# Strassen's algorithm on a third row pair of eight in the first MLP product

## The chip, the cores and the metric

The kernel runs on one core of a Trainium2 chip. TensorE (PE in the profile) multiplies matrices, with its weight loads shown apart (PEld); VectorE (DVE) and ScalarE (ACT) do elementwise work; GpSimd (POOL) and SyncE (SP) mostly start DMA transfers. The metric is the device time of one execution in microseconds, lower is better; a time given for a kernel is the median of several runs.

## What is computed

A trunk of two layers over 256 tokens of width 2048, in float32. Each layer has an attention half and an MLP half; the change is in the MLP half:

```python
for l in range(DEPTH):                     # DEPTH = 2
    u = rmsnorm(x, norm_mix[l])
    ...                                    # two kinds of attention, gated and merged
    x = x + merged @ w_out[l]
    h = rmsnorm(x, norm_mlp[l]) @ w_ff1[l]          # 2048 -> 8192
    x = x + jnp.square(jax.nn.relu(h)) @ w_ff2[l]   # 8192 -> 2048
return rmsnorm(x, norm_final)
```

## The kernel before

**Precision.** Every float32 factor is split into a high part (rounded to the format that TensorE multiplies fast, by a cast on ScalarE) and a low part (the remainder, by a subtraction on VectorE). A product is then three matmuls: high by high, high by low, low by high. In the MLP half `parts` does the split of weights (L172 the cast, L173 the subtraction), into tiles `hi` and `lo` of which there are three each.

**The MLP half.** It goes through four blocks `b` (L775) of 2048 hidden columns. A block is four calls of `gemm_s` (L368): the first product for column half `g` = 0 and 1 (L788), then the second product for the output halves 0 and 1 (L806); in the last block the second half is done by `gemm_a` instead (L816). A call of `gemm_s` computes 256 rows by 1024 columns with 2048 contracted, in eight steps called row pairs: a pair `j` is 256 rows of the weight, one DMA of 1 MB into `raw` (L391, three buffers), against 2 x 2 blocks of the activations.

A plain pair casts its 128x2048 weights in one piece and does 8 block products of three matmuls each, 24 matmuls of 512 columns (L399, all matmuls on L383). They go into four PSUM banks, numbers 2, 3, 4 and 8. A pair named in `pairs` is done by Strassen's algorithm (in Winograd's form): VectorE builds four sums of the weight's quarters (`ts`, L405 to L411, one buffer), the three quarters that are used as they stand and the four sums are split (L412, L413, so two `hi` and two `lo` tiles in place of one), and there are 7 block products, 21 matmuls, into banks 1 to 7:

```python
w11, w22, w21 = cut(raw[:, 512:])
w1, w3, w2, w4 = cut(ts)
...
mm3(1, a11, l11, *w11)
mm3(2, a12, l12, *w21)
mm3(3, s4, r4, *w22)
mm3(5, s1, r1, *w1)
mm3(7, s3, r3, *w3)
mm3(6, s2, r2, *w2)
mm3(4, a22, l22, *w4)
```

The first three use the first `hi`/`lo` tile, the last four the second. All eight PSUM banks are in use in a call. At its end ScalarE copies bank 1 (L427) and VectorE adds the other banks up in eight additions (L428 to L435, recorded as L426) to four result tiles.

**Activations.** `turned_pair` (L339) transposes four 128x128 blocks on TensorE (L346) into a bank, takes them to SBUF (for hidden rows by ScalarE's square, L786), and splits them (L360, L361). For a pair that goes by Strassen it first forms four sums of 128x128 on VectorE (L352 to L355) and splits these too; its high and low parts then take four tiles from the pool `slots` in place of two. This is done once per layer for the eight pairs of normed rows (L758) and in every block for the eight pairs of hidden rows (L785). Pieces of such work are held as generators and handed out between the matmuls by `tick` (L125), a count of steps with due times; `drain` (L144, called at L404 ahead of the first Strassen pair) hands out all that is left.

**Order.** The program's own order gives priorities; a planner that knows the cost of instructions then fixes the order in each engine's queue when the kernel is built. At run time each queue goes in that order and waits on semaphores.

**Constants.** `FIRST` and `SECOND` (L65) name the Strassen pairs of the first and of the second product. `NSLOT` (L62) is the number of 128x512 tiles in `slots`, which hold activations, hidden rows and results. `SMALL` is the number of tiles of 128x256 tagged `small` (L96), which exist in the attention half alone: `whole` (L236) takes two to bring an accumulator out of PSUM (L238, L240), `rope` (L463) and `Norm.add` (L296) one each. A `slots` tile takes 2 KB of a partition, a small tile 1 KB.

Of the kernel before, what the change touches and what calls it, by code (L numbers as in the profile page):

```python
# [58 lines left out]

NSLOT, SMALL, RBUFS, HBUFS = 46, 8, 3, 4  # L62


FIRST, SECOND = (3, 5), (2, 4, 6)  # L65


SPACING, LAG1, LAG2 = 6, 13, 3
# [822 lines left out]
```

## Time and profile before

| | |
|---|---|
| median of 3 runs | 2675.92 us (2674.61 to 2676.1) |
| the profiled execution | 2675.85 us |
| its span, first to last instruction | 2674.1 us |
| instructions on TensorE, VectorE, ScalarE | 12606, 2172, 1611 |
| matmuls on L383, the MLP's `gemm_s` | 5538 (3692 with a high part, 1846 with a low part of the weight) |
| DMA traffic | 508.92 MB, 190 GB/s |

The profile is of one execution. Its rows give for each engine the line of the kernel, the tile written and the tiles read, the shape and the count; then the busy time, the mean of one in ns, and the time for which the engine stood idle just before such an instruction, with what ended the wait behind an arrow. A timeline row begins with the start in microseconds and the duration. The first layer's attention half lasts to 643.8 us, its MLP half from there to about 1338; the second layer follows in the same way.

### The profile page before, as it was taken

The page shows a single profiled execution, that of the slowest core. Times are in us where ns is not written, and L with a number is a line of the kernel's source. Part 1 is how long each engine was busy: PE and PEld are TensorE (multiplying, and loading weights), DVE is VectorE, ACT ScalarE, POOL GpSimd, SP SyncE. Part 2 cuts the span into 40 slices and gives each one's busy share as a digit, 9 for nine tenths or more (in the row PEclk, how much of TensorE's full clock was granted, in tenths as well). Part 3 has the DMA queues.
Part 4 walks back from the last instruction along what each step waited for, and adds up shares of the span by engine and source line. Part 5 has one row for each costly group of instructions (what it writes and reads, how often), then busy time and mean ns, then how long its engine had stood idle before and what let it go on. Part 6 is the DMA issues. An engine that isn't in the chain of part 4 may idle for free.

```text
span 2674.1 us, 31697 instructions
## 1 busy us (share of the span) xinstructions
PE 2636.0 (99%) x12606; PEld 2206.9 (83%) x12606; DVE 1912.9 (72%) x2172; ACT 1388.7 (52%) x1611; POOL 95.4 (4%) x122
## 2 busy tenths in 40 slices
PE   8999999999999999999999999999999999999998
PEld 7888888878888888888888888888788888888886
DVE  5675486556788887888667654955568888878885
ACT  5554464445555545546445544644455555455553
POOL 1100000000000010000001000000000000100000
PEclk9999999999999999999999999999999999999999
DMA  7555644555667585675555555455655665766754
GB/s 233 185 156 190 195 152 157 189 189 167 206 194 237 169 241 193 201 235 176 186 179 179 163 188 185 147 170 172 202 169 200 204 220 179 237 204 199 252 168 147
DMA packets 199301, 508.92 MB, mean 190 GB/s; under 512 B 13457, under 2 KB 17553, under 8 KB 199153
## 3 DMA queue, kind: packets, MB, share of 16 engines
q1 hardware_dynamic: 189184, 488.14, 55.6%
q0 software_dynamic: 8960, 17.14, 3.2%
q8 instruction: 98, 1.61, 0.2%
q10 hardware_dynamic: 1008, 1.61, 0.2%
q14 instruction: 51, 0.41, 0.0%
HBM read 492.18 MB, written 2.10 MB: 185 GB/s over the span
## 4 chain that ended last, share of the span: by engine, by line
PE 85%; issue 7%; DVE 5%; ACT 2%; DMA 1%; POOL 0%; POOLq 0%; DVEq 0%; ACTq 0%
PE bank L383 36%; PE bank L228 11%; PE bank L229 11%; PE bank L227 11%; PE bank L218 8%; PE bank L219 4%; DVE lo L173 2%; ACT hi L172 2%; PE bank L346 1%; PE bank L232 1%; PE bank L234 1%; PE bank L233 1%; DVE pair L361 1%; PE bank L496 0%; DMA raw<-in_w_in 0%
## 5 line engine op out<-in xcount | busy, mean ns | idle before, releaser
L383 PE MATMUL bank<-hi,pair 128*128 128x512 f32 x3692 | 1147.3, 390 | 4.3 <-ACT hi L172 3.3
L383 PEld LDWEIGHTS bank<-hi,pair 128*128 128x128 f32 x3692 | 691.8, 188 | 153.7 <-ACT hi L172 11.0
L173 DVE TENSOR_TENSOR lo<-raw,hi 128x2048 fp32r<-128x2048 f32 (+1 forms) x288 | 618.3, 2150 | 184.9 <-ACT hi L172 183.8
L172 ACT CAST hi<-raw 128x2048 fp32r<-128x2048 f32 (+1 forms) x288 | 517.5, 1802 | 442.0 <-PE bank L383 254.5
L383 PE MATMUL bank<-lo,pair 128*128 128x512 f32 x1846 | 720.0, 390 | 0.0
L197 DVE TENSOR_TENSOR lo<-raw,hi 128x1024 fp32r<-128x1024 f32 (+1 forms) x352 | 427.6, 1217 | 343.4 <-ACT hi L196 342.8
L196 ACT CAST hi<-raw 128x1024 fp32r<-128x1024 f32 (+1 forms) x352 | 364.5, 1041 | 402.9 <-PE bank L229 291.6
L228 PE MATMUL bank<-lo,pair 128*128 128x512 f32 (+1 forms) x1344 | 518.5, 386 | 2.4 <-DVE lo L173 2.4
L227 PE MATMUL bank<-hi,pair 128*128 128x512 f32 (+1 forms) x1344 | 518.9, 387 | 0.0
L229 PE MATMUL bank<-hi,pair 128*128 128x512 f32 (+1 forms) x1344 | 518.1, 386 | 0.0
L383 PEld LDWEIGHTS bank<-lo,pair 128*128 128x128 f32 x1846 | 346.6, 188 | 72.8 <-DVE lo L173 1.8
L218 PE MATMUL bank<-pair,hi 128*128 128x512 f32 x960 | 346.3, 403 | 4.2 <-ACT hi L196 3.8
L228 PEld LDWEIGHTS bank<-lo,pair 128*128 128x128 f32 x1344 | 253.4, 189 | 51.5 <-DVE lo L173 2.9
L229 PEld LDWEIGHTS bank<-hi,pair 128*128 128x128 f32 x1344 | 253.4, 189 | 50.7
L227 PEld LDWEIGHTS bank<-hi,pair 128*128 128x128 f32 x1344 | 253.1, 188 | 49.1
L219 PE MATMUL bank<-pair,lo 128*128 128x256 f32 x960 | 266.9, 282 | 0.0
L173 DVE TENSOR_TENSOR lo<-sums,hi 128x2048 fp32r<-128x2048 f32 x74 | 169.6, 2292 | 112.9 <-ACT hi L172 112.9
L172 ACT CAST hi<-sums 128x2048 fp32r<-128x2048 f32 x74 | 141.5, 1912 | 185.5 <-DVE sums L411 154.5
L218 PEld LDWEIGHTS bank<-pair,hi 128*128 128x128 f32 x960 | 181.2, 189 | 43.6 <-ACT hi L196 4.2
L219 PEld LDWEIGHTS bank<-pair,lo 128*128 128x128 f32 x960 | 181.9, 190 | 1.7
L426 DVE TENSOR_TENSOR wide<-wide,bank 128x512 f32<-128x512 f32 x240 | 153.9, 679 | 0.0
L407 DVE TENSOR_TENSOR sums<-raw 128x1024 f32<-128x1024 f32 x74 | 90.2, 1219 | 11.7 <-DMA raw<-in_w_ff 11.4
(122 smaller groups left out, 1463.6 us busy)
## 6 DMA issues: line engine op xcount, KB each, us to landing
raw<-in_w_ff SPq DMA_DIRECT2D x256, 1024.0 KB, 5.3
raw<-in_w_in SPq DMA_DIRECT2D x124, 1024.0 KB, 5.1
raw<-in_w_out SPq DMA_DIRECT2D x32, 1024.0 KB, 5.0
raw<-in_w_o_na SPq DMA_DIRECT2D x16, 1024.0 KB, 5.0
raw<-in_w_o_mla SPq DMA_DIRECT2D x16, 1024.0 KB, 5.0
xt<-wide POOLq DMA_DIRECT2D x48, 256.0 KB, 7.1
raw<-in_w_ukv SPq DMA_DIRECT2D x8, 1024.0 KB, 4.9
raw<-in_w_uq SPq DMA_DIRECT2D x8, 768.0 KB, 4.5
```

The costliest lines, as they stand in the source:

```text
L172: nc.scalar.copy(hi, src)
L173: nc.vector.tensor_tensor(lo, src, hi.bitcast(F32), op=ALU.subtract)
L196: nc.scalar.copy(hi, src)
L197: nc.vector.tensor_tensor(lo, src, hi.bitcast(F32), op=ALU.subtract)
L218: nc.tensor.matmul(ps, wh, a, start=first, stop=False)
L219: nc.tensor.matmul(ps[:, :S], wl, a[:, :S], start=False, stop=last)
L227: nc.tensor.matmul(ps, ah, wh, start=first, stop=False)
L228: nc.tensor.matmul(ps, ah, wl, start=False, stop=False)
L229: nc.tensor.matmul(ps, al, wh, start=False, stop=last)
L383: nc.tensor.matmul(b[i], x, y, start=count[i] == 1, stop=count[i] == total[i])
L407: nc.vector.tensor_tensor(ts[:, :1024].rearrange("p (a n) -> p a n", a=2), raw[:, :512].rearrange("p (a n) -> p a n", a=1).to_broadcast([P ...
L426: add = lambda o, a, c: nc.vector.tensor_tensor(o, a, c, op=ALU.add)
```

## The change

Pair 6 of the first product joins pairs 3 and 5 as a Strassen pair. Two constants move with it: two more tiles in `slots` and four fewer small tiles, the same 4 KB of a partition.

```diff
-NSLOT, SMALL, RBUFS, HBUFS = 46, 8, 3, 4
+NSLOT, SMALL, RBUFS, HBUFS = 48, 4, 3, 4
...
-FIRST, SECOND = (3, 5), (2, 4, 6)
+FIRST, SECOND = (3, 5, 6), (2, 4, 6)
```

`FIRST` is used at L759, where the normed rows of its pairs get their sums, and at L788, where `gemm_s` takes the pairs. No other line changes.

## The prediction

> **What bounds the kernel now.** I read the page first, then the busy time by stage, the chain of waits, and the queues of VectorE and ScalarE where that chain leaves TensorE. The page says how full TensorE is:
>
> ```profile
> span 2674.1 us, 31697 instructions
> PE 2636.0 (99%) x12606; PEld 2206.9 (83%) x12606; DVE 1912.9 (72%) x2172; ACT 1388.7 (52%) x1611; POOL 95.4 (4%) x122
> ```
>
> TensorE idles 38 us in all, but 99% is an average. By stage: one of the four MLP blocks of a layer (first line), and the up-projections of the latent attention (second):
>
> ```profile
> 864.50:1036.60 172.10, 171.55 (x772) 141.55 (x771) 141.63 (x128) 92.42 (x73) 7.07 (x8) 1.00 0.65 208
> ...
> 350.00:405.00 55.00, 54.23 (x369) 49.85 (x368) 53.08 (x126) 36.68 (x87) 0.00 (x0) 1.00 0.48 154
> ```
>
> The columns are the stretch, then busy time of PE, PEld, DVE, ACT and POOL, the granted clock (1.00) and the DMA share. In the MLP VectorE is busy 141.6 of 172.1 us; in the attention stretch 53.1 of 55.0, a second limit beside TensorE. The chain of waits prices a matmul and shows where TensorE isn't alone:
>
> ```profile
> 738.58 1.75 PE bank L346 x16
> ...
> 743.56 1.92 ACT hi L172
> ...
> 765.86 1.91 ACT hi L172
> ...
> 767.81 96.65 PE bank L383 x425
> ```
>
> 96.65 us over 425 matmuls is 0.227 us from one 512-column matmul to the next (one matmul's own duration is longer, since they overlap; the step is what counts). Sixteen transposes cost 1.75. A block has 2 x 186 + 2 x 183 = 738 matmuls of L383 and 32 transposes: 738 x 0.227 + 2 x 1.75 = 171.0 us of 172.1, so about 1.1 us of a block is waiting. It falls early in the second product, where the chain leaves TensorE and runs over ScalarE and VectorE, from 743.56 to 767.81. ScalarE's and TensorE's own rows there:
>
> ```profile
> 752.24 0.62 ACT L360 CAST pair<-f 128x512 fp32r<-128x512 f32 x1 [0.94 <-DVE f L354]
> 752.76 1.91 ACT L172 CAST hi<-sums 128x2048 fp32r<-128x2048 f32 x1
> ```
> ```profile
> 757.16 0.97 PE L383 MATMUL bank<-hi,pair 128*128 128x512 f32 x3 [0.42 <-ACT hi L172]
> ```
>
> A cast of sums stood behind a small cast that waited; TensorE then waited too.
>
> **What goes.** A Strassen pair takes 21 matmuls where a plain one takes 24. There are 2 layers x 4 blocks x 2 column halves = 16 such products, so 48 matmuls go: 48 x 0.227 = **10.9 us**, 0.68 per product. Nothing hides them: the stretch is full of them.
>
> The Trainium skill ("TensorE: Matmul & The Clock Gate", Back-to-back issue gap) gives about 131 ns per 512-column matmul in a sustained stream of weight loads and matmuls, and about 216 for isolated ones. By 131 the saving would be 6.3 us, by 216 10.4; the trace's 227 for this very instruction stands against the first and near the second.
>
> **What is added to each of the 16 products.** VectorE and ScalarE prepare pair 6 as two tiles in place of one:
>
> ```profile
> L173 DVE TENSOR_TENSOR lo<-raw,hi 128x2048 fp32r<-128x2048 f32 x22 | 50.3, 2286 | 9.3 <-ACT hi L172 9.2
> L173 DVE TENSOR_TENSOR lo<-sums,hi 128x2048 fp32r<-128x2048 f32 x10 | 22.9, 2292 | 15.1 <-ACT hi L172 15.1
> L426 DVE TENSOR_TENSOR wide<-wide,bank 128x512 f32<-128x512 f32 x32 | 20.5, 678 | 0.0
> L173 DVE TENSOR_TENSOR lo<-raw,hi 128x1536 fp32r<-128x1536 f32 x10 | 17.5, 1752 | 2.1 <-ACT hi L172 2.1
> L407 DVE TENSOR_TENSOR sums<-raw 128x1024 f32<-128x1024 f32 x10 | 12.2, 1219 | 1.6 <-DMA raw<-in_w_ff 1.6
> L411 DVE TENSOR_TENSOR sums<-raw,sums 128x512 f32<-128x512 f32 x11 | 7.6, 688 | 0.2
> L361 DVE TENSOR_TENSOR pair<-f,pair 128x512 fp32r<-128x512 f32 x11 | 7.4, 686 | 2.0 <-ACT pair L360 2.0
> ```
> ```profile
> L172 ACT CAST hi<-raw 128x2048 fp32r<-128x2048 f32 x22 | 42.1, 1914 | 28.3 <-PE bank L383 28.3
> L172 ACT CAST hi<-sums 128x2048 fp32r<-128x2048 f32 x10 | 19.1, 1912 | 26.9 <-DVE sums L411 23.2 <-PE bank L383 3.6
> L172 ACT CAST hi<-raw 128x1536 fp32r<-128x1536 f32 x10 | 14.8, 1483 | 16.0 <-DVE sums L410 6.0 <-DMA raw<-in_w_ff 4.0 <-PE bank L383 4.0
> ```
>
> VectorE: 1.22 + 0.69 + 0.69 for the sums (L410 taken as L411, the same form), 1.75 + 2.29 for the low parts, less 2.29: **4.34 us more**. ScalarE: 1.48 + 1.91 - 1.91 = 1.48 more. Over a block VectorE then has 141.6 + 8.7 = 150.3 us in 170.7: 88%, still under TensorE. DMA is unchanged: the same megabyte a pair.
>
> So the sum hangs on whether 4.34 us fit locally. The second product with column half 0 already runs three Strassen pairs of eight beside the splitting of hidden rows, and waits about 1 us; the first product, half 1, would carry that load, but with pairs 5 and 6 adjacent. Its queue before:
>
> ```profile
> 717.48 2.29 DVE L173 TENSOR_TENSOR lo<-raw,hi 128x2048 fp32r<-128x2048 f32 x1 [3.23 <-ACT hi L172]
> ...
> 728.15 1.23 DVE L407 TENSOR_TENSOR sums<-raw 128x1024 f32<-128x1024 f32 x1 [1.58 <-DMA raw<-in_w_ff]
> ...
> 738.34 2.29 DVE L173 TENSOR_TENSOR lo<-sums,hi 128x2048 fp32r<-128x2048 f32 x1 [1.50 <-ACT hi L172]
> ...
> 745.51 2.29 DVE L173 TENSOR_TENSOR lo<-raw,hi 128x2048 fp32r<-128x2048 f32 x1 [1.13 <-ACT hi L172]
> ```
> ```profile
> 715.54 1.91 ACT L172 CAST hi<-raw 128x2048 fp32r<-128x2048 f32 x1 [3.61 <-PE bank L383]
> 717.35 0.57 ACT L427 COPY wide<-bank 128x512 f32<-128x512 f32 x1
> ```
>
> There are three hi and three lo buffers, so a cast waits for TensorE to finish the tile three places back. At 715.54 pair 4 is finished and pair 6 may be cast. Pair 5's first tile is finished 9 matmuls later (717.6), its second 12 after that (720.3). With the change: the three sums of pair 6 fit in VectorE's 3.23 us before 717.48 (they need 2.6). First tile of pair 6: cast 715.54 to 717.0, low part to 718.8. Second: cast 717.6 to 719.5, low part to 721.8; TensorE gets there at 720.3 + 2.04 = 722.3, so 0.5 us is spare. Pair 7: cast 720.3 to 722.2, low part to 724.5; wanted at 725.0, again 0.5 spare. Of the idle time to 738.34 (3.23 + 1.58 + 1.50 = 6.31 us) 4.34 is used; 2 us and the 1.13 before 745.51 remain, while TensorE arrives 0.68 earlier. I take **nothing** for the wait; if the cover is gone it is the 4.34, once per block.
>
> Behind pair 6's three sums on VectorE stand the low parts of pair 7 and the accumulator adds (L426). The adds move: banks 1, 5, 6 and 7 now finish with pair 6, about 5 us before the product's end, where pair 5 gave them 10. Four adds of 0.68 fit in 5 us. The next weight load starts about 2 us later, since its buffer is freed by pair 7's low part.
>
> Half 0 has the same gap and no hidden rows to split:
>
> ```profile
> 845.59 2.29 DVE L173 TENSOR_TENSOR lo<-raw,hi 128x2048 fp32r<-128x2048 f32 x1 [3.33 <-ACT hi L172]
> ```
>
> Once per layer pair 6 of the normed rows gets four sums of 128x128, a cast and a split more (each no more than the 0.686 of L361, whose form is four times as wide as those sums: under 3.5 us of VectorE), some 30 us before they are used: nothing, or 7 us uncovered. NSLOT's two more hold the second pair of its tiles.
>
> **SMALL 8 to 4** touches only the attention half. There an evacuation takes two small tiles through copy, add, multiply, cast and subtract:
>
> ```profile
> L238 ACT COPY small<-bank x20: 352/374/394, 352.0 to 403.2; 128x256 f32<-128x256 f32 x20
> L240 DVE TENSOR_TENSOR small<-bank,small x20: 401/416/424, 352.9 to 404.8; 128x256 f32<-128x256 f32 x20
> L162 ACT ACTIVATE pair<-small x19: 409/417/452, 355.5 to 403.8; 128x256 fp32r<-128x256 f32 x19
> ```
>
> That is 0.37 + 3 x 0.42 + 0.42 = 2.05 us, and 20 come in 55 us, one per 2.75. Four tiles allow two at once, one while the rotary tile holds its place; so the rate suffices and only queueing can cost. Bounds: zero below (fewer buffers add waits, they remove none), and above a wait of one cast (0.42) on VectorE for each of 20, less the 1.9 us it idles there: 6.5 per layer, 13 in all. I take 1.5 for both layers: the rate argument puts it near the lower end.
>
> **Sum.** The profiled execution took 2675.85 us (its span and 1.75 around it), 0.07 under the median of the three runs. 2675.85 - 10.9 + 1.5 = **2666.5 us**.
>
> **Rivals.** *The spare is lost (0.14).* The copy L427 waits for bank 1, whose last matmuls now are the first three of pair 6, at 720.3 + 0.68. If ScalarE's queue has the copy (0.57) ahead of pair 7's cast, that cast starts at 721.55 in place of 720.3: 1.25 late against 0.5 spare, 0.75 lost in each of 16 products, 12 us, and the time is 2675.85 - 10.9 + 12 + 1.5 = 2678.5. For it: the row of 717.35, where the copy stands ahead of pair 7's cast, and the cast at 752.76, held up behind one that waited. Against: in the second product, where pair 6 is Strassen already, the copy stands behind pair 7's cast:
>
> ```profile
> 765.86 1.90 ACT L172 CAST hi<-raw 128x2048 fp32r<-128x2048 f32 x1
> 767.67 0.57 ACT L427 COPY wide<-bank 128x512 f32<-128x512 f32 x1
> ```
>
> The Trainium skill (the same page, the row Engine queue depth of its first table) calls ScalarE's and VectorE's queues strict first-in-first-out. By that rule a copy put ahead does hold the cast up; the 752.24 row agrees.
>
> *VectorE takes over (0.11), slower.* If the planned order leaves the gaps before 738 unused and only the 1.13 before 745.51 is, VectorE enters the second product 4.34 - 1.13 = 3.2 us late, where the chain of waits already runs over it and TensorE has no lead: 8 x 3.2 = 25.7 us, 2675.85 - 10.9 + 25.7 + 1.5 = 2692. It decides for slower from about 1.85 us of new waiting per block (8 x 1.85 = 14.8 = 10.9 + 5.4 - 1.5). For it: VectorE's queue was already on the chain there. Against: 20 of a block's 170.7 us stay free on VectorE, and the 3.23 us gap lies right where pair 6's sums can go.
>
> *The small tiles cost their bound (0.05):* 2675.85 - 10.9 + 13 = 2678.
>
> That the matmuls don't go is excluded by the code.
>
> **Numbers.** 0.70 for the forecast. A change under 0.2% (5.35 us) can't be told from none. Faster: the forecast and a little of the first rival, should it strike in few products, 0.72; same: the rest of it and the third, 0.17; slower 0.11. The range is 2663 (no cost of the small tiles, and 2 of the 9 us of waiting in eight blocks gone with a new order) to 2679, which takes in the first and third rivals; the second is left out.
>
> **What would show it.** TensorE instructions down by 48 in L383; L407 16 times more often; a block about 1.4 us shorter, 170.7; VectorE about 150 in it. Wrong, if TensorE waits on ACT hi or DVE lo L173 in pairs 6 or 7 (first rival), more than 2 us a block in the second product (second), or if 350 to 405 grows by over 2 us (third).

## The result and the profile after

The changed kernel takes 2706.89 us (median of 4 runs, 2703.77 to 2708.18) where the kernel before takes 2676.01: a ratio of 1.0115 [1.0104, 1.0127]. It is 31 us slower; 9.5 us less had been forecast. The page of after, whose profiled execution took 2703.77 us:

```profile
span 2702.0 us, 31714 instructions
PE 2634.9 (98%) x12558; PEld 2194.5 (81%) x12558; DVE 1987.0 (74%) x2246; ACT 1412.2 (52%) x1629; POOL 94.8 (4%) x122
...
L383 PE MATMUL bank<-hi,pair 128*128 128x512 f32 x3660 | 1145.8, 392 | 25.2 <-ACT hi L172 25.2
...
L383 PE MATMUL bank<-lo,pair 128*128 128x512 f32 x1830 | 715.0, 392 | 6.3 <-DVE lo L173 6.3
```

The 48 matmuls are gone (12606 to 12558), and the last numbers of the two L383 rows have grown: TensorE stands idle 31.5 us ahead of them. The view of TensorE's waits (total, times, longest) names what it waited for, which in before came to 3.3 us in 8 waits of at most 0.4:

```profile
PE bank L383 <- ACT hi L172: 25.2, 30, 1.6
PE bank L383 <- DVE lo L173: 6.3, 8, 0.9
```

Where it happens, by stage. Call the four products of an MLP block F0, F1 (the first product, column halves 0 and 1), S0 and S1 (the second product's). The windows view of before and of after, each first F1 and then S0 of the first block (columns as in the prediction: stretch, length, then busy time of PE, PEld, DVE, ACT, POOL with instruction counts, clock, DMA share, GB/s):

```profile
686.70:730.70 44.00, 44.00 (x203) 36.58 (x202) 34.37 (x33) 25.70 (x24) 0.00 (x0) 1.00 0.56 191
730.70:775.20 44.50, 43.95 (x200) 35.82 (x199) 37.95 (x41) 27.84 (x26) 0.00 (x0) 1.00 0.53 166
```
```profile
684.70:730.80 46.10, 43.92 (x200) 35.82 (x200) 38.62 (x36) 27.34 (x25) 0.00 (x0) 1.00 0.53 174
730.80:778.70 47.90, 44.76 (x200) 35.56 (x199) 40.81 (x45) 28.00 (x26) 0.00 (x0) 1.00 0.55 181
```

F1 has three matmuls fewer and is 2.1 us longer; S0 has the same matmuls and is 3.4 us longer (the first block's S0 is the worst of the eight). To have this for all eight blocks I took from the traces the start of every matmul of L383, subtracted 0.227 us a step (0.109 for a transpose), and added up what is left from the first matmul of a product to the first of the next, which is good to about 0.1 us. This *loss* is 0.09 us in F1 and 1.28 in S0 of before, in each block. In after it is 25.8 us over the eight F1 (2.84 in six of them, 4.3 and 4.45 in two) and 25.3 over the eight S0 (1.7 to 4.7); F0 and S1 lose nothing in either kernel. (The loss is larger than the idle time of the rows: it also holds what a matmul's own 0.39 us covers of a wait, and single steps of 0.31 to 0.52 us before and after a stop.) Against before that is 25.1 + 15.0 = 40.1 us of new waiting, less 10.9 for the matmuls gone, less 1.3 by which the first MLP begins earlier: 27.9 us, and the two spans differ by 2702.0 - 2674.1 = 27.9. (The medians differ by 30.9: the profiled run of after is its fastest.)

What F1 waits for is seen in VectorE's queue there (the timeline of after; in brackets the idle time ahead of a row and what ended it):

```profile
707.85 1.75 DVE L173 TENSOR_TENSOR lo<-raw,hi 128x1536 fp32r<-128x1536 f32 x1
709.52 0.69 DVE L411 TENSOR_TENSOR sums<-raw,sums 128x512 f32<-128x512 f32 x1
712.23 2.29 DVE L173 TENSOR_TENSOR lo<-sums,hi 128x2048 fp32r<-128x2048 f32 x1 [2.03 <-ACT hi L172]
715.08 1.76 DVE L173 TENSOR_TENSOR lo<-raw,hi 128x1536 fp32r<-128x1536 f32 x1 [0.55 <-ACT hi L172]
716.75 1.22 DVE L407 TENSOR_TENSOR sums<-raw 128x1024 f32<-128x1024 f32 x1
718.01 0.69 DVE L410 TENSOR_TENSOR sums<-raw,sums 128x512 f32<-128x512 f32 x1
718.74 0.69 DVE L411 TENSOR_TENSOR sums<-raw,sums 128x512 f32<-128x512 f32 x1
721.60 2.29 DVE L173 TENSOR_TENSOR lo<-sums,hi 128x2048 fp32r<-128x2048 f32 x1 [2.17 <-ACT hi L172]
```

The cast and the matmul that belong to it, in the timelines of ScalarE and of TensorE:

```profile
719.18 0.59 ACT L427 COPY wide<-bank 128x512 f32<-128x512 f32 x1 [4.14 <-PE bank L383]
719.67 1.90 ACT L172 CAST hi<-sums 128x2048 fp32r<-128x2048 f32 x1
```
```profile
721.62 1.19 PE L383 MATMUL bank<-hi,pair 128*128 128x512 f32 x4 [1.57 <-ACT hi L172]
```

Read it backwards. TensorE wants pair 6's cast sums at 721.62 - 1.57 = 720.05 and gets them 1.57 us late. The cast could not start before the last sum (L411, done at 719.4); the copy L427 ahead of it, in ScalarE's queue, can have cost it at most the 0.24 us from there to 719.67. The sums started at 716.75, behind pair 6's *raw* split, which itself had waited for its cast. They could not have started before 714.5 in any case: there is one tile for the sums, and until then pair 5's sums were being split. That split is itself late. The same place in before:

```profile
709.22 0.68 DVE L411 TENSOR_TENSOR sums<-raw,sums 128x512 f32<-128x512 f32 x1
709.82 1.75 DVE L173 TENSOR_TENSOR lo<-raw,hi 128x1536 fp32r<-128x1536 f32 x1
711.96 2.29 DVE L173 TENSOR_TENSOR lo<-sums,hi 128x2048 fp32r<-128x2048 f32 x1 [0.39 <-ACT hi L172]
```

Here pair 5's last sum (L411) stands ahead of pair 5's raw split, in after behind it. Counted from the start of F1 (686.7 in before, 684.7 in after) the split of pair 5's sums ends at 27.5 us in before and at 29.8 in after. So pair 6's sums are late by 2.3 us through pair 5's, and by 2.2 more (714.5 to 716.75) through pair 6's raw split. Why the planner chose this order these runs do not show. So two chains of differences on VectorE, cast on ScalarE, split on VectorE run one behind the other, and VectorE, from 710 to 721.6, is *idle* for 2.03 + 0.55 + 2.17 = 4.75 us while TensorE comes to a stop.

In half 0 the same operations stand in another order, the sums of pair 6 directly behind the split of pair 5's, and nothing is lost:

```profile
666.54 2.29 DVE L173 TENSOR_TENSOR lo<-sums,hi 128x2048 fp32r<-128x2048 f32 x1 [0.85 <-ACT hi L172]
668.86 1.22 DVE L407 TENSOR_TENSOR sums<-raw 128x1024 f32<-128x1024 f32 x1
...
671.73 1.76 DVE L173 TENSOR_TENSOR lo<-raw,hi 128x1536 fp32r<-128x1536 f32 x1 [0.19 <-ACT hi L172]
```

### The profile page after: what moved, and what is told of

It is laid out like the page before. It is cut to its first block, busy times and chain, and to the rows that moved or that the text cites. A ratio compares the mean times of both kernels' runs of the same rounds, so it can differ in the third digit from the quotient of the medians.

```text
span 2702.0 us, 31714 instructions
## 1 busy us (share of the span) xinstructions
PE 2634.9 (98%) x12558; PEld 2194.5 (81%) x12558; DVE 1987.0 (74%) x2246; ACT 1412.2 (52%) x1629; POOL 94.8 (4%) x122
## 4 chain that ended last, share of the span: by engine, by line
PE 78%; issue 15%; DVE 4%; ACT 2%; DMA 1%; POOL 1%; POOLq 0%; DVEq 0%; ACTq 0%
PE bank L383 30%; PE bank L229 10%; PE bank L228 10%; PE bank L227 10%; PE bank L218 8%; PE bank L219 4%; DVE lo L173 2%; ACT hi L172 1%; PE bank L346 1%; PE bank L232 1%; PE bank L234 1%; PE bank L233 1%; DMA raw<-in_w_in 0%; PE bank L496 0%; POOL xt L800 0%
## 5 line engine op out<-in xcount | busy, mean ns | idle before, releaser
L383 PE MATMUL bank<-hi,pair 128*128 128x512 f32 x3660 | 1145.8, 392 | 25.2 <-ACT hi L172 25.2
L383 PEld LDWEIGHTS bank<-hi,pair 128*128 128x128 f32 x3660 | 684.4, 188 | 181.8 <-ACT hi L172 40.2
L383 PE MATMUL bank<-lo,pair 128*128 128x512 f32 x1830 | 715.0, 392 | 6.3 <-DVE lo L173 6.3
L172 ACT CAST hi<-raw 128x2048 fp32r<-128x2048 f32 (+1 forms) x288 | 510.3, 1779 | 402.2 <-PE bank L383 210.2
L173 DVE TENSOR_TENSOR lo<-raw,hi 128x2048 fp32r<-128x2048 f32 (+1 forms) x288 | 609.3, 2121 | 123.9 <-ACT hi L172 123.6
L383 PEld LDWEIGHTS bank<-lo,pair 128*128 128x128 f32 x1830 | 344.2, 188 | 83.0 <-DVE lo L173 10.9
L173 DVE TENSOR_TENSOR lo<-sums,hi 128x2048 fp32r<-128x2048 f32 x90 | 206.3, 2292 | 141.9 <-ACT hi L172 141.9
L172 ACT CAST hi<-sums 128x2048 fp32r<-128x2048 f32 x90 | 172.0, 1911 | 189.1 <-DVE sums L411 148.0
L407 DVE TENSOR_TENSOR sums<-raw 128x1024 f32<-128x1024 f32 x90 | 109.8, 1220 | 1.8 <-DMA raw<-in_w_ff 1.2
```

The costliest lines, as they stand in the source:

```text
L172: nc.scalar.copy(hi, src)
L173: nc.vector.tensor_tensor(lo, src, hi.bitcast(F32), op=ALU.subtract)
L383: nc.tensor.matmul(b[i], x, y, start=count[i] == 1, stop=count[i] == total[i])
L407: nc.vector.tensor_tensor(ts[:, :1024].rearrange("p (a n) -> p a n", a=2), raw[:, :512].rearrange("p (a n) -> p a n", a=1).to_broadcast([P ...
```

## The experiments

The expectations name these theories. **A**: pairs 5 and 6 side by side share one sums tile. **B**: VectorE has too much to do over the whole block. **C**: the four small tiles. **P**: any newly planned order of the queues costs this much. **D**: what decides is VectorE's load in F1 and S0, where hidden rows are split too (rows 0 to 3 in F1, rows 4 to 7 in S0). Later D was cut in two: **V**, VectorE has too little *time* in F1; **O**, the *order* of its queue through the one sums tile is to blame. The losses in us per block (mean over the blocks, worked out as above), with the times:

| kernel | median us | ratio to before [95%] | F0 | F1 | S0 | S1 |
|---|---|---|---|---|---|---|
| before | 2676.01 | | 0.0 | 0.1 | 1.3 | 0.0 |
| after | 2706.89 | 1.0115 [1.0104, 1.0127] | 0.0 | 3.2 | 3.2 | 0.0 |
| e1 constants alone | 2675.74 | 1.0003 [0.9994, 1.0012] | 0.0 | 0.1 | 1.3 | 0.0 |
| e2 first pairs 2, 4, 6 | 2683.35 | 1.0035 [1.0022, 1.0048] | 0.0 | 1.7 | 2.2 | 0.0 |
| e3 first pairs 5, 6 | 2683.36 | 1.0031 [1.0020, 1.0043] | 0.0 | 0.0 | 2.5 | 0.0 |
| e4 two sums tiles | 2685.93 | 1.0044 [1.0029, 1.0059] | 2.4 | 0.1 | 1.3 | 0.0 |
| e5 third pair in half 0 only | 2669.75 | 0.9978 [0.9969, 0.9986] | 0.0 | 0.1 | 1.3 | 0.1 |
| e6 hidden low parts on GpSimd | 2706.43 | 1.0112 [1.0097, 1.0128] | 0.0 | 0.8 | 6.2 | 0.0 |
| e7 the same in before | 2690.66 | 1.0056 [1.0043, 1.0070] | 0.0 | 0.2 | 2.9 | 0.0 |
| e9 second pairs 4, 6 | 2664.21 | 0.9958 [0.9946, 0.9971] | 0.0 | 0.1 | 0.1 | 0.0 |
| e10 before, second pairs 4, 6 | 2675.78 | 1.0003 [0.9994, 1.0013] | 0.0 | 0.1 | 0.1 | 0.0 |
| e11 second pairs 2, 6 | 2690.11 | 1.0055 [1.0041, 1.0069] | 0.2 | 3.2 | 0.2 | 0.0 |
| e12 e4 with one sums tile | 2713.21 | 1.0138 [1.0125, 1.0152] | 0.0 | 3.8 | 3.5 | 0.0 |
| e13 sums split first, all pairs | 2708.85 | 1.0128 [1.0111, 1.0145] | 1.5 | 1.5 | 3.0 | 1.4 |
| e14 the same in before | 2671.21 | 0.9985 [0.9976, 0.9995] | 0.0 | 0.0 | 0.7 | 0.4 |
| e15 sums split first, pair 6 | 2684.93 (1 run) | | 0.1 | 0.5 | 3.0 | 0.4 |

**e1: the constants without the third pair.**

```
-NSLOT, SMALL, RBUFS, HBUFS = 46, 8, 3, 4
+NSLOT, SMALL, RBUFS, HBUFS = 48, 4, 3, 4
 FIRST, SECOND = (3, 5), (2, 4, 6)
```

> Only the two constants are changed (48 slots, 4 small tiles); the first product keeps pairs 3 and 5. Theory A (pairs 5 and 6 are adjacent and share one tile for the sums of the weights, so VectorE can't form pair 6's sums before pair 5's are split) and theory B (VectorE has 8.7 us more of work per block, whichever pairs carry it) both expect 2676, within 3 us. Theory C (fewer small tiles cost the time) expects 2690 to 2707.

2675.74 us, no difference. Theory C falls. The interval (-1.6 to +3.2 us) does not exclude the prediction's 1.5 us, but the traces show no such cost: TensorE's first matmul of L383 comes at 642.3 us in after and at 643.6 in before, and from the last one of the first layer to the first of the second it is 679.1 us in after and 679.2 in before.

**e2 and e3: three pairs that are not neighbours; two pairs that are.**

```
-FIRST, SECOND = (3, 5, 6), (2, 4, 6)
+FIRST, SECOND = (2, 4, 6), (2, 4, 6)      # e2
```
```
-FIRST, SECOND = (3, 5), (2, 4, 6)
+FIRST, SECOND = (5, 6), (2, 4, 6)         # e3, from before and its constants
```

> Three Strassen pairs of eight in the first product, as in the change, but pairs 2, 4 and 6, none beside another. Theory A expects the matmuls' saving to show: 2665 to 2670, with blocks of about 171 us. Theory B expects the time of the change, 2700 to 2710, with blocks of about 177 us.

> Two Strassen pairs in the first product as before, with the constants of before, but adjacent: 5 and 6 in place of 3 and 5. The work of every engine is that of before. Theory A expects the wait inside pair 6 of the first product again, 2 to 4 us a block: 2692 to 2707. Theory B expects 2676, within 3 us.

Both fell between the theories. Three pairs set apart still lose 1.7 us in F1; two neighbours lose nothing in F1, but make S0 worse by 1.2. Neighbourhood alone is not the cause, nor is the number of pairs alone.

**e4 and e12: a second tile for the sums, and its control.** To make room, e4 also keeps the sums of hidden rows in a tile of their own (one buffer), two diagonal tiles for four, and takes the norm's scratch tile from the wide ones; lines below shift by 3 (L407 is L410). e12 has all of this and one sums tile.

```
-            ts = wpool.tile([P, 2048], F32, tag="sums", name="sums", bufs=1)
+            ts = wpool.tile([P, 2048], F32, tag="sums", name="sums", bufs=2)
```

> The change with two tiles for the sums of the weights in place of one (room for it is made by a junk tile from the pool of slots, the activations' sums in a tile of their own, and two diagonal tiles in place of four). Theory A expects the sums of pair 6 ahead of its split, no wait there, and most of the saving: 2665 to 2680. Theory B expects 2700 to 2710.

> The kernel with two tiles for the sums (2685.93 us) with one tile again and everything else of its memory kept (the sums rows of hidden pairs in a tile of their own, two diagonal tiles for four, the norm's scratch tile from the wide ones). If the second sums tile was what took the loss out of the second half of the first product: 2707 us, as after, with 2.8 us a block lost there. If the other memory edits did it: 2686 us.

e4 took 2685.93 us, 6 more than theory A allowed for and far from B's 2700. The control, 2713.21, is as slow as after or slower, with 3.8 us lost in F1: so the second tile by itself takes F1's loss away (3.8 to 0.1), and S0's falls to 1.3 with it. But a new loss of 2.4 us appears in F0. VectorE's and TensorE's timelines in e4:

```profile
825.21 1.76 DVE L173 TENSOR_TENSOR lo<-raw,hi 128x1536 fp32r<-128x1536 f32 x1 [0.88 <-ACT hi L172]
830.82 1.22 DVE L410 TENSOR_TENSOR sums<-raw 128x1024 f32<-128x1024 f32 x1 [3.85 <-DMA raw<-in_w_ff]
...
836.02 1.23 DVE L410 TENSOR_TENSOR sums<-raw 128x1024 f32<-128x1024 f32 x1 [0.45 <-DMA raw<-in_w_ff]
...
838.62 2.28 DVE L173 TENSOR_TENSOR lo<-raw,hi 128x2048 fp32r<-128x2048 f32 x1
```
```profile
840.96 0.50 PE L386 MATMUL bank<-lo,pair 128*128 128x512 f32 x1 [2.56 <-DVE lo L173]
```

With a tile free, the queue has the next pairs' differences early, where they wait 3.85 and 0.45 us for loads; the split at 838.62, for which TensorE waits 2.56 us, stands behind them. The queues run in order: the Trainium skill says so of ScalarE's and VectorE's ("TensorE: Matmul & The Clock Gate", row Engine queue depth of the first table), and these rows agree.

**e5: the third pair in column half 0 alone.**

```
-                gemm_s(w_ff1[l], b * D + g * 1024, xg, FIRST, relu2)
+                gemm_s(w_ff1[l], b * D + g * 1024, xg, FIRST[:3 - g], relu2)
```

> The change in column half 0 of the first product alone: three Strassen pairs there (3, 5, 6), two (3, 5) in half 1, where VectorE also splits hidden rows. Theory D (the new work is free in half 0 and costs in half 1 and right after it, because VectorE splits the hidden rows there) expects the 24 matmuls' 5.4 us as a gain: 2670, within 2 us, blocks of 171.5. Theory P (any new planned order costs, wherever the pair is put) expects 2680 or more.

2669.75 us, 0.9978 [0.9969, 0.9986]: faster than both kernels, and as theory D had it. Half the matmuls go (24 x 0.227 = 5.4 us) and all new loss goes. Theory P falls: this order is new too.

**e6 and e7: the low parts of the hidden rows on GpSimd**, in after and in before.

```
-            nc.vector.tensor_tensor(lw, src, h.bitcast(F32), op=ALU.subtract)
+            eng.tensor_tensor(lw, src, h.bitcast(F32), op=ALU.subtract)   # gpsimd for hidden rows
```

> The change, with the low parts of the hidden rows (L361, for those rows alone) subtracted on GpSimd in place of VectorE: 11 instructions of 0.69 us a block off VectorE, about 3.4 us of them in half 1 of the first product and 4.1 right after it. Theory D expects the loss in half 1 gone or under 1 us and the second product's no worse than before: 2660 to 2675. Theory P expects 2695 to 2710.

> The same move to GpSimd in the kernel before. Theory D expects at most the 1.2 us a block that TensorE waits in the second product: 2666 to 2676. Theory P has no number; a time above 2680 would speak for it, since no engine that bounds gets more work.

A miss as a test: e6 took 2706.43 us where theory D expected 2660 to 2675, and e7 2690.66 where it expected at most 2676. The groups of GpSimd's instructions, of e7 and of e6:

```profile
L361 POOL TENSOR_TENSOR pair<-f,pair 128x512 fp32r<-128x512 f32 x88 | 149.0, 1708 | 685.0 <-ACT pair L360 407.0 <-PE bank L346 260.1 <-issue 17.8
```
```profile
L361 POOL TENSOR_TENSOR pair<-f,pair 128x512 fp32r<-128x512 f32 x88 | 187.2, 2145 | 653.5 <-ACT pair L360 359.6 <-PE bank L346 263.4 <-issue 30.5
```

It takes 1.71 and 2.15 us on the mean for what VectorE does in 0.69, and the move alone costs before 15 us, 13 of them in S0 (1.6 us a block more). F1's loss did fall, 3.2 to 0.8, but so much else changed that this tells nothing apart.

**e8 to e11: lighter hidden rows.** A hidden row pair in SECOND needs four sums of 128x128 and a second split; pair 2's fall in F1, pair 4's in S0. Each pair dropped also adds 42 matmuls (9.5 us). e8 and e9 are one kernel, once and in five rounds; e10 is its control, from before with the constants of after.

```
-FIRST, SECOND = (3, 5, 6), (2, 4, 6)
+FIRST, SECOND = (3, 5, 6), (4, 6)       # e8, e9
+FIRST, SECOND = (3, 5), (4, 6)          # e10
+FIRST, SECOND = (3, 5, 6), (2, 6)       # e11
```

> The change, with pair 2 of the second product plain again: 42 matmuls more (9.5 us), and 1.8 us less of VectorE in half 1 of the first product (the hidden pair 2 needs no sums) and 4.3 less in each second product. Theory D expects the loss in half 1 to fall from 2.8 to under 1.5 us a block and that in the second product's half 0 from 3.4 to under 1.5. Theory P expects both to stay above 2.

> The kernel after with two row pairs (4, 6) in the second product, as one single run gave 2662.62 us; now for an interval. Theory D (what decides is VectorE's work while hidden rows are split): 2662.6 us again, ratio to before 0.995. If that single run was luck or another chip's: 2670 or more.

> The kernel before (two pairs in the first product, the tile counts of after) with two pairs (4, 6) in the second product. It adds 42 matmuls x 0.227 = 9.5 us and should take the 1.28 us that the first half of the second product loses in before down to 0.1, x 8 = 9.4 us. Theory D: 2675 to 2676 us, so that the third pair is worth its whole 10.9 to 13 us once the hidden rows are lighter. If two pairs in the second product are a gain by themselves that has nothing to do with the third pair: 2666 us or less.

> The kernel after with the pairs (2, 6) in the second product: as many matmuls and as much VectorE work in all as with (4, 6), but the heavy hidden pair 2, whose rows are split in the second half of the first product, stays, and pair 4, whose rows are split in the first half of the second product, goes. Theory D by stages: the loss of 2.84 us a block in the second half of the first product stays and the second product's goes, 2662.6 + 8 x 2.8 = 2685 us. If the total of VectorE's work decides: 2663 us, as with (4, 6).

e8 took 2662.62 us, e9 2664.21: 11 us below before in the same runs (2674.78), 43 below after, with 42 matmuls more than after. e10 took 2675.78, so the two pairs in the second product are no gain by themselves. e10 and e9 lose the same 0.1 in F1 and S0, and differ by 11.6 us: the third pair is worth its 48 matmuls, whole, once nothing waits. e11, with the same number of matmuls and of VectorE's operations as e9, takes 26 us more, and 25 of them are F1's loss of 3.2 us a block, back unchanged. That excludes B, and D was right about the place. The windows view of F1 in e9 and in e11:

```profile
684.50:727.80 43.30, 43.30 (x201) 35.97 (x200) 38.05 (x32) 27.07 (x24) 0.00 (x0) 1.00 0.56 191
```
```profile
685.10:731.00 45.90, 43.73 (x200) 35.66 (x200) 38.33 (x36) 27.34 (x25) 0.00 (x0) 1.00 0.52 172
```

VectorE does 38.05 us of work in 43.30 us and nothing is lost; it does 38.33 in e11, and 2.8 us are. So its load hardly decides there; look at the order. VectorE's timeline in e9:

```profile
709.86 2.29 DVE L173 TENSOR_TENSOR lo<-sums,hi 128x2048 fp32r<-128x2048 f32 x1 [0.37 <-ACT hi L172]
712.19 1.23 DVE L407 TENSOR_TENSOR sums<-raw 128x1024 f32<-128x1024 f32 x1
713.45 0.69 DVE L410 TENSOR_TENSOR sums<-raw,sums 128x512 f32<-128x512 f32 x1
714.17 0.69 DVE L411 TENSOR_TENSOR sums<-raw,sums 128x512 f32<-128x512 f32 x1
714.97 1.76 DVE L173 TENSOR_TENSOR lo<-raw,hi 128x1536 fp32r<-128x1536 f32 x1
717.21 2.29 DVE L173 TENSOR_TENSOR lo<-sums,hi 128x2048 fp32r<-128x2048 f32 x1 [0.49 <-ACT hi L172]
```

The split of pair 5's sums is as early here as in before, and the queue has pair 6's sums directly behind it, as in half 0. They are done at 714.9, 30.4 us after the start of F1 (684.5); in after it is 34.7 us (719.4 less 684.7).

**e13 to e15: the order alone.** Two lines of after change places, for all pairs (e13), and for pair 6 alone, in both products (e15); e14 is e13's edit in before. No instruction is added or removed.

```
-            w11, w22, w21 = cut(raw[:, 512:])
             w1, w3, w2, w4 = cut(ts)
+            w11, w22, w21 = cut(raw[:, 512:])
```

> The kernel after with two lines changed about: each Strassen pair's sums are written (and so planned) ahead of the split of its raw weights. Not one instruction is added or taken away. In the planned order of VectorE's queue in the second half of the first product, the first difference of pair 6 then stands right behind the split of pair 5's sums, where in after the raw split of pair 6 stands between. Theory O (the order of VectorE's queue through the one sums tile): the 2.84 us a block in that half goes, 2.84 x 8 = 23 us less, and 2684 us or less depending on what the new order does in the second product. Theory V (VectorE has too little time while the heavy hidden rows are split): the work is the same, so 2700 to 2710 us stay.

> The same two lines changed about in the kernel before, as the control: the new order by itself. In before only the first half of the second product loses (1.28 us a block). If the new order is as good there: 2676 us; if it takes that loss too: 2666 us; if the raw split comes late now: 2680 us or more.

> The kernel after with the sums ahead of the raw split in pair 6 alone. Theory O: the loss of the first product's second half goes as with all pairs, 2684 us or less; theory V: 2700 to 2710 us.

e15 settles F1: 2684.93 us in its single run, 22 below after. Its F1 in the windows view, and VectorE's timeline:

```profile
685.40:729.10 43.70, 43.70 (x200) 35.82 (x200) 38.91 (x38) 27.14 (x25) 0.00 (x0) 1.00 0.53 179
```
```profile
711.02 2.28 DVE L173 TENSOR_TENSOR lo<-sums,hi 128x2048 fp32r<-128x2048 f32 x1
713.34 1.22 DVE L407 TENSOR_TENSOR sums<-raw 128x1024 f32<-128x1024 f32 x1
```

VectorE is busy 38.91 us in it, not less than after's 38.62, and the stage takes 43.70 in place of 46.10. The sums of pair 6 again start directly behind the split of pair 5's. Theory V falls for F1, theory O holds. e13 is the warning: by its time alone, 2708.85 us, it looks like theory V. The same exchange in all pairs halves F1's loss, but F0 and S1, which lost nothing, now lose 1.5 and 1.4, and TensorE waits 18.6 us on low parts (`DVE lo L173`) where after has 6.3. In before, that same order is 4 us faster (e14, 0.9985 [0.9976, 0.9995]).

**S0 is settled in part.** Its loss goes from 1.3 to 2.2 or more in most kernels whose F1 carries more (e2, e15, after), and in e3; it goes to 0.1 when one of the second product's three pairs is dropped (e9 to e11). e15 kept 3.0 there, with VectorE busy 40.7 of 46.2 us. The amount of work does not explain that loss. The windows view of S0 in the first block of e4 and of its control e12 has:

```profile
729.96:774.53 44.57, 43.92 (x200) 35.81 (x199) 40.48 (x44) 27.77 (x26) 0.00 (x0) 1.00 0.58 192
731.86:778.90 47.04, 45.22 (x201) 35.53 (x200) 40.53 (x46) 27.75 (x26) 0.00 (x0) 1.00 0.54 178
```

VectorE does the same 40.5 us in both, and with two tiles for the sums the stage is 2.5 us shorter and loses 1.3, as in before. (In this block e4 loses nothing in F0 and F1 either, so no earlier stop of TensorE gave VectorE a lead.) So the second tile, with the order that it allows, takes away S0's new loss as well. What stays open is which step of S0's queue costs it, and why the order that cured F1 in e15 left S0 as it was.

## Why the prediction was wrong, point by point

- **48 matmuls x 0.227 = 10.9 us: right.** e10 less e9 gives 11.6 us for them, 0.24 each. The Trainium skill's 131 ns a matmul ("TensorE: Matmul & The Clock Gate", Back-to-back issue gap) would give 6.3; these runs speak against it.
- **4.34 us more of VectorE a product: right in amount.** Its busy time in a block went from 141.6 to 150.2 us (150.3 forecast):

```profile
695.52:872.51 176.99, 171.67 (x765) 140.05 (x765) 150.17 (x135) 95.42 (x76) 7.09 (x8) 1.00 0.64 204
```

- **The step that failed: "the three sums of pair 6 fit in VectorE's 3.23 us before 717.48 (they need 2.6)", and so "I take nothing for the wait".** In half 0 the sums do go there. In half 1 they do not, and TensorE waits 2.8 us for them in most blocks. The step took the place of everything else from the queue of before, where the split of pair 5's sums ends at 711.96 + 2.29 = 714.25, just as the 3.23 us begin, so that the one sums tile is free. But the queue is planned anew with the change. In after pair 5's sums are 2.3 us later, the one tile holds pair 6's sums back until they are split, and pair 6's raw split, which waits for its own cast, stands ahead for 2.2 us more. Neither the tile count of the sums nor a new order stood in any step of the sum; of the rivals only the second had the order as its condition. In S0, where 1.9 us a block of new waiting arise, the prediction expected none either; that the one tile matters there e4 and e12 show, the exact step they do not.
- **"If the cover is gone it is the 4.34, once per block": the price was near.** 40.1 us of new waiting over eight blocks is 5.0 a block, 3.1 in F1 and 1.9 in S0. By 4.34 the time would have been 2675.85 - 10.9 + 34.7 = 2699.7 us. What was wrong was to call it covered. That the price is near is partly luck: 4.34 us is the length of the added work, and in F1 the wait came from order, with that work unchanged in e15.
- **1.5 us for the small tiles:** no run shows it (e1 and the traces above). The third rival was no case.
- **The first rival** (the copy L427 ahead of a cast) is not what happened: the copy stands ahead of the cast at 719.67, but that cast waited for the sums until 719.4, and at most 0.24 us can be the copy's. TensorE does wait on ACT hi and DVE lo in pairs 6 and 7, as this rival's sign had it: the sign did not separate the two rivals.
- **The second rival**, slower at 2692, was the nearest in direction and in its condition (the gaps stay unused). It placed the loss in the second product only, where 15 us of it arose; 25 came in F1. It does not say the cause either: in F1 VectorE was not the bound but waited. At 0.11 it was left out of the range; the argument against it, 20 us free on VectorE in a block, is one about averages, which the prediction itself warned of.

## What to carry to other kernels

Before filling an engine's idle time with new work, ask whether the buffer that the work writes is free by then, and whether the queue, planned anew, will have the work in that place. In half 0, in e9 and in e15 the gap was room, and the sums went into it. In after the order and the one buffer put two chains (differences, cast, split) one behind the other, and 4.75 us of idle time were waits inside them. So a new operation has to be followed through its buffer and its queue stage by stage, since the same edit cost nothing in half 0 and 3.2 us a block in half 1. When the loss is found, try the order alone, and drop work where it stands in the way: one Strassen pair fewer in the second product made the third pair of the first worth its full 11.6 us.

## What the hardware showed besides

In two of after's eight blocks F1 loses 1.5 us more than the 2.84 of the others, for the same two waits. The windows view of after, in the stretch behind such a stall and the one after it:

```profile
1076.20:1080.20 4.00, 4.00 (x11) 3.13 (x12) 4.00 (x3) 1.72 (x1) 0.00 (x0) 0.57 0.32 76
1080.20:1084.00 3.80, 3.80 (x18) 3.15 (x17) 3.77 (x5) 1.92 (x1) 0.00 (x0) 1.00 0.81 284
```

The granted clock is 0.57 for 4 us; single matmuls there start 0.43 us apart in place of 0.227, as TensorE's timeline has them:

```profile
1077.69 0.63 PE L383 MATMUL bank<-hi,pair 128*128 128x512 f32 x1
1078.12 0.63 PE L383 MATMUL bank<-lo,pair 128*128 128x512 f32 x1
```

TensorE had stood still for 1.57 and 0.61 us with four matmuls between. The Trainium skill ("TensorE: Matmul & The Clock Gate", Part 1: The HAM clock gate) has the clock halve after an idle window of some 3.4 us; here a shorter stall was enough, in two blocks of eight. So a stall can cost its stage more than its length. What the block loses is another matter: in the first of the two blocks S0 then lost 1.7 us in place of 3.0 to 3.5, so that F1 and S0 together lost 6.1, as in the blocks without the slow clock (5.9 to 6.3; the first block 7.5). In the second they lost 7.0.

GpSimd's subtraction of 128x512 took 1.71 us on the mean in e7 and 2.15 in e6, against VectorE's 0.69.
